# Hybrid decoder step: thirty 0/1-matrix sums as two products of a split operand, triangle matrices without their zero blocks, HGRN level products written together

## The chip, the cores and the metric

The kernel runs on one core of a Trainium2 chip. The metric is the device time of one execution in microseconds (us); lower is better. One execution was also profiled, and every row quoted below comes from it.

## The reference, cut to what matters

One trunk layer over 320 rows (256 of a prompt, 64 of eight samples), width 2048. All large matrices are float32.

```python
hn = rms_norm(x, norm_mix);  proj = hn @ w_in            # 2048 -> 6656 columns, three head groups
# A) RWKV-7: 12 heads of 64; delta rule with decay, in chunks here
kk = kf * k_k;  kk = kk / max(sqrt(sum(kk*kk, axis=-1)), 1e-12)          # sum over the 64 rows of a head
S = S*w + (S @ a) b^T + v k^T;  y = S @ r
mean = y.mean(-1); var = ((y-mean)**2).mean(-1)                           # sums over 64 rows
bonus = sum(r * k * r_k, axis=-1) * v                                     # sum over 64 rows
# B) HGRN2: 6 heads, 128 x 128 state
o = q exp(b) S + tril(q exp(b_t - b_s) k) v;  o = rms_norm(o, norm_w)     # sum over the 128 rows of a head
# C) RG-LRU: 512 channels
x = x + concat(y_rw, y_hg, y_lru) @ w_out
x = x + (silu(conv(gate)) * val) @ w_down                                 # gated MLP, width 5632
```

## The kernel before, in words

Data lies transposed: features on the 128 partitions, the 320 rows of tokens along the free dimension. Every large product is made exact enough by splitting: weights and activations are each cut into a rounded part (float32r) and the remainder, and a chunk of eight 128 x 128 weight tiles gives 24 products of 320 columns: high by high and low in turn (L198, L199), then low weights by high (L205). ScalarE (ACT) rounds the weights (L173), VectorE (DVE) subtracts (L174), SyncE (SP) loads them (L167).

The first third of the span ("the mixing stage") interleaves these products of `w_in` with the recurrences. The helper chains are Python generators: `tick` is called after every eight products and at a chunk's end, and lets a chain write its next step once the planner's clock has advanced by the amount that the chain yielded (`L_HG`, `L_EV`, `L_ST` and so on, in units near a microsecond). TensorE (PE) runs in the written order, apart from small shifts that the tile framework makes by readiness; every engine works its own queue in order.

The pieces that the change touches:

- **Sums over rows.** A sum over 64 or 128 partitions, broadcast back, is a product with a constant 0/1 matrix from the constant block `cst`: `bones` (same half of 64), `bswap` (other half), `ones`. There are five per pair of RWKV heads or HGRN head, six times: L502 (norm of k), L663 (bonus), L825 and L832 (mean and variance), L1019 (HGRN norm). These are products of plain float32 operands, 128 x 128 by 128 x 320. The three others with `ones` (L401, L1226, L1280 and L1281) sum over all features.
- **The triangle inverse.** Each RWKV pair needs the inverse of four 128 x 128 unit triangles that hold two 64 x 64 blocks, in tiles `mt1`, `Us`, `Ts`, `Z`. The 16 x 16 diagonal blocks are inverted by 30 small DVE instructions in sequence (L611, L613), for which `mt1` goes out to DRAM and comes back as blocks (L606, L607) and the result goes back the same way (L614, L615, all four from SP's queue). Then `Us` is transposed on PE (L686), and two levels of block products (L703) merge 16 to 32 and 32 to 64. Each such product has a 64 x 64 stationary block and 64 moving columns, of which half are zero by construction. ACT copies to `Z` (L708), DVE writes back under a mask (`update`, L695).
- **The chunk steps of RWKV.** Four chunks follow each other (L781, L784, L785 on PE; ACT and DVE make the state `sbd` in between at L792, L794), spaced by `L_ST`.
- **HGRN levels.** The intra-chunk matrix `at` of a head is filled level by level (h = 2, 4, ..., 64): `pairs` makes two or three products per level (L913, L917), each followed by its masked copy into `at` (L914, L918), all in one PSUM tile.
- **Transposes of v and kd** of a head go through a small tile `both` (L983), one buffer for each.

Of the kernel before, what the change touches and what calls it, by code (L numbers as in the profile page):

```python
# [51 lines left out]
CST = {}  # L52
_n = 0
for _name, _w in (
    ("ident", 128), ("ones", 128), ("bones", 128), ("bswap", 128), 
    ("psw", 128), ("eye2", 64), ("bmx", 4), ("bm4", 4), ("sel", 64), ("bm2", 2),
):
    CST[_name] = (_n, _w)
    _n += _w
# [7 lines left out]
def kernel(ctx: ExitStack, tc: tile.TileContext, i: dict, o: dict):  # L67
# [16 lines left out]
    prm = cp.tile([P, NPRM], F32, tag="prm", name="prm")  # L84
    cst = cp.tile([P, NCST], F32, tag="cst", name="cst")
    msk = cp.tile([P, NMSK], U8, tag="msk", name="msk")

    def pc(name, n, rows=slice(0, P)):
        c = PRM[name] + n
# [245 lines left out]
    G.memset(m01[:, 260:332:9], 0.0)  # L335

    ident = cc("ident")
    ones = cc("ones")

    def tok8(ap):  # L340
        return ap.rearrange("p (b t) -> p b t", t=ST)
# [100 lines left out]
        G.memset(t, 0.0)  # L442


    Zs = [mp.tile([P, 4, P], F32, tag=f"Z{h}", name=f"Z{h}") for h in (16, 32)]
    for Z in Zs:
        G.memset(Z, 0.0)

# [25 lines left out]
    def rwkv_operands(p, lw, box):  # L474
        while state["pairs"] < p - 1:
            yield None
        if p == 0:
            yield L_FIRST

        ps_w, ps_a = aux_r(), aux_r()  # L480
        for n, ps in enumerate((ps_w, ps_a)):
            PE.matmul(ps[:, :T], lw[half[n], n, :], lora[half[n], :], start=True, stop=True)  # L482
        sw = ft("sw")
        G.memset(sw[:, 0:260:65], 0.0)
        G.memset(sw[:, 260:332:9], 0.0)
        swp = sw[:, 0:260].rearrange("p (c s) -> p c s", s=65)
        sws = sw[:, 260:332].rearrange("p (c s) -> p c s", s=9)
        S.activation(swp[:, :, 1:65], ps_w[:, 0:TP].rearrange("p (c s) -> p c s", s=64), AF.Sigmoid,
                     bias=pc("w0", p))
        S.activation(sws[:, :, 1:9], tok8(ps_w[:, TP:T]), AF.Sigmoid, bias=pc("w0", p))  # L490
        a = ft("a", T)
        S.activation(a, ps_a[:, :T], AF.Sigmoid, bias=pc("a0", p))
        cum = ft("cum")
        V.tensor_tensor_scan(cum, m01, sw, 0.0, op0=ALU.mult, op1=ALU.add)
        while "k" not in box:
            yield None
        k, k_own = box["k"]
        kn = ft("kn", T)
        S.activation(kn, k, AF.Square, scale=pc("kk", p))
        yield L_K  # L500
        ps_k = aux_r()
        PE.matmul(ps_k[:, :T], cc("bones"), kn, start=True, stop=True)  # L502
        V.tensor_scalar(kn, ps_k[:, :T], 1e-24, None, op0=ALU.max)
        S.activation(kn, kn, AF.Ln, scale=float(2 ** 20))
        S.activation(kn, kn, AF.Exp, scale=-0.5, bias=eps_pow)  # L505
        ep = ft("ep")
        S.activation(ep, cum, AF.Exp, scale=-KAPPA)
        en = cum
        S.activation(en, cum, AF.Exp, scale=KAPPA)
        V.scalar_tensor_tensor(kn, k, pc("kk", p), kn, op0=ALU.mult, op1=ALU.mult)  # L510
        nb = ft("nb", T)
        V.scalar_tensor_tensor(nb, kn, -1.0, a, op0=ALU.mult, op1=ALU.mult)
        k2 = a
        V.tensor_scalar(k2, a, -1.0, pc("ka", p), op0=ALU.add, op1=ALU.mult)
# [48 lines left out]
    def rwkv_chunks(p, lw, box):  # L563
# [96 lines left out]
        state["samples"] += 1  # L660
        yield L_FILL
        ps_b = aux_r()
        PE.matmul(ps_b[:, :T], cc("bswap"), rk, start=True, stop=True)  # L663
        bo = ct("bo", T)
        V.tensor_tensor(bo, ps_b[:, :T], v, op=ALU.mult)
        free(v_own)
# [21 lines left out]
        for h, Z in zip((16, 32), Zs):  # L688
            def part(t, j):

                return t.rearrange("p b (n j s) -> p b n j s", j=2, s=h)[:, :, :, j, :]

            def update(t, name, j, ps):
                m = part(mask(name).unsqueeze(1), j)
                V.copy_predicated(part(t, j), m.to_broadcast([P, 4, 64 // h, h]),  # L695
                                  ps[:, 0:256].rearrange("p (b n s) -> p b n s", b=4, s=h))

            def blocks(ps, lhs, rhs, j):

                for b in range(4):  # L700
                    r = part(rhs[:, b:b + 1, :], j)
                    for q in half:
                        PE.matmul(ps[q, b * 64:(b + 1) * 64], lhs[q, b, q], r[q], start=True, stop=True)  # L703

            yield L_EV
            ps = aux_r()
            blocks(ps, mt1[:, 0], Ts, 0)
            S.copy(part(Z, 0), ps[:, 0:256].rearrange("p (b n s) -> p b n s", b=4, s=h))  # L708
            yield L_EV
            ps_u = aux_r()  # L710
            blocks(ps_u, Z, Us, 1)
            if h == 16:
                ps_t = aux_r()
                blocks(ps_t, Us, Z, 0)
            update(Us[:, 0:4, :], f"u{h}", 1, ps_u)
            if h == 16:
                update(Ts, "t16", 0, ps_t)

# [102 lines left out]
    def rwkv_norm(p, lw, y, bo):  # L821
        yield L_NORM

        ps_m = aux_r()
        PE.matmul(ps_m[:, :T], cc("bones"), y, start=True, stop=True)  # L825
        yc = ct("yc", T)
        V.scalar_tensor_tensor(yc, ps_m[:, :T], -1.0 / 64, y, op0=ALU.mult, op1=ALU.add)
        sq = ct("sqy", T)
        S.activation(sq, yc, AF.Square)
        yield L_EV  # L830
        ps_v = aux_r()
        PE.matmul(ps_v[:, :T], cc("bones"), sq, start=True, stop=True)  # L832
        lnv = sq
        S.activation(lnv, ps_v[:, :T], AF.Ln, scale=1.0 / 64, bias=eps_ln)
        S.activation(lnv, lnv, AF.Exp, scale=-0.5)
# [41 lines left out]
    def hgrn_steps(n, box):  # L877
# [28 lines left out]
        def pairs(lhs, rhs, h, w):  # L906

            ps = aux_h()
            for c0 in range(0, w, P):
                c = slice(c0, min(c0 + P, w))  # L910
                n = c.stop - c0
                if h == 2:
                    PE.matmul(ps[0:n, c], lhs[:, c], rhs[:, c], start=True, stop=True)  # L913
                    V.copy_predicated(at[0:n, c], mask("u2")[0:n, 0:n], ps[0:n, c])  # L914
                else:
                    o = ps[0:n, c0 // 2:(c0 + n) // 2]
                    PE.matmul(o, lhs[:, c], halves(rhs[:, c], n, h)[1], start=True, stop=True)  # L917
                    V.copy_predicated(halves(at[0:n, c], n, h)[1], halves(mask(f"u{h}")[0:n], n, h)[1],  # L918
                                      o.rearrange("p (n s) -> p n s", s=h))

# [56 lines left out]
        vt = rp.tile([P, 3, P], F32, tag="vt", name="vt", bufs=1)  # L977
        kt = rp.tile([P, 3, P], F32, tag="kt", name="kt", bufs=1)

        both = []  # L980
        for src in (v, kd):
            t = rp.tile([P, 2, TS], F32, tag="both", name="both", bufs=2)
            G.tensor_copy(t, bcast(src[:, TP:T], 2))  # L983
            both.append(t)
        for src, t, dst in ((v, both[0], vt), (kd, both[1], kt)):
            yield L_HG
            ps = aux_h()
            for m in range(2):
# [27 lines left out]
        S.activation(sq, ps_o[:, :T], AF.Square)  # L1016
        yield L_EV
        ps_n = aux_h()
        PE.matmul(ps_n[:, :T], ones, sq, start=True, stop=True)  # L1019
        rs = ht("hrs", T)  # L1020
        S.activation(rs, ps_n[:, :T], AF.Ln, scale=1.0 / P, bias=eps_norm)
        S.activation(rs, rs, AF.Exp, scale=-0.5)
# [278 lines left out]
L_NORM = 2.5  # L1301
L_FILL = 1.0
L_EV = 1.5
L_ST = 0.5
L_END = 0.5
L_HG = 2.0
L_HG0 = 12.0
# [23 lines left out]
def _constants():  # L1331
# [6 lines left out]
        c[:, CST[name][0]:CST[name][0] + CST[name][1]] = a.reshape(P, -1)  # L1338

    put("ident", (s == t).astype(f))  # L1340
    put("ones", np.ones((P, P), f))
    put("bones", (s // 64 == t // 64).astype(f))
    put("bswap", (s // 64 != t // 64).astype(f))
    s6 = (r % 64)[:, None]
    t6 = np.arange(64)[None, :]
    strict, causal = s6 < t6, s6 <= t6
# [120 lines left out]
```

## Time and profile before

| | |
|---|---|
| time, median of 3 runs | 1633.42 us (1631.91 to 1633.76) |
| the profiled execution: its own time | 1633.52 us |
| its span (first to last instruction) | 1631.8 us, so 1.7 us lie around it |
| granted TensorE clock | 0.997 |
| ACT table loads | 87, 111.6 us in all |
| DMA | 238.91 MB, mean 146 GB/s |

A matmul's row shows when it started and how long it took until its last result; since matmuls are pipelined, what one costs is the distance of starts, not its length. A plain float32 product appears as two records, a float32r product as one. "PEld" is the loading of stationary operands, which runs ahead of the products.

### The profile page before, as it was taken

What the parts mean: (1) busy time and instruction counts of PE and PEld (TensorE: products, weight loads), DVE (VectorE), ACT (ScalarE), POOL (GpSimd) and SP (SyncE); (2) the same over time, 40 slices, a digit from 0 to 9 for tenths busy, and PEclk for the clock granted to TensorE, in tenths of its full rate; (3) what the DMA queues carried; (4) which work ended last, traced back from release to release, by engine and by line L of the source; (5) the groups of instructions that cost most, each with busy time, mean ns of one, the idle gap of its engine ahead of it and who ended that gap; (6) DMA issues with size and microseconds to landing.
All of it is one profiled execution on the core that took longest, in us unless ns stands there. A gap on an engine that the chain in (4) does not pass through costs nothing.

```text
span 1631.8 us, 28987 instructions
## 1 busy us (share of the span) xinstructions
PE 1604.3 (98%) x11478; PEld 1549.6 (95%) x11478; DVE 984.9 (60%) x1965; ACT 821.9 (50%) x1289; POOL 147.9 (9%) x364
## 2 busy tenths in 40 slices
PE   9999999999999999999999999999999999999996
PEld 8888988888889999999999999999999999999996
DVE  7777787777777665555555554434555555554444
ACT  7766666767676774443443433332343443344442
POOL 2101110101011300011111100000011110010000
PEclk9999999999999999999999999999999999999998
DMA  7444342525353554444544445555444444545553
GB/s 267 151 131 133 119 137 92 159 94 158 96 153 114 166 165 153 153 152 147 155 146 152 147 150 146 151 148 151 155 155 145 153 145 154 154 147 156 146 153 108
DMA packets 87792, 238.91 MB, mean 146 GB/s; under 512 B 16713, under 2 KB 31097, under 8 KB 87657
## 3 DMA queue, kind: packets, MB, share of 16 engines
q1 hardware_dynamic: 81496, 221.01, 44.1%
q0 software_dynamic: 4576, 14.16, 2.6%
q8 instruction: 90, 1.47, 0.4%
q10 hardware_dynamic: 1584, 1.89, 0.3%
q14 instruction: 46, 0.37, 0.1%
HBM read 225.66 MB, written 11.37 MB: 145 GB/s over the span
## 4 chain that ended last, share of the span: by engine, by line
PE 89%; DVE 5%; ACT 4%; issue 1%; DMA 1%; SPq 0%; DVEq 0%; ACTq 0%
PE acc L198 27%; PE acc L205 27%; PE acc L199 26%; DMA raw<-in_w_in 1%; PE aux_r L703 1%; PE aux_h L917 1%; DVE wl L174 1%; ACT wh L173 0%; DVE x L1287 0%; PE aux_h L913 0%; PE aux_h L1046 0%; PE aux_r L781 0%; ACT L505 0%; PE aux_r L482 0%; PE aux_r L578 0%
## 5 line engine op out<-in xcount | busy, mean ns | idle before, releaser
L173 ACT CAST wh<-raw 128x1024 fp32r<-128x1024 f32 (+2 forms) x412 | 421.5, 1024 | 515.2 <-PE acc L199 310.9
L198 PE MATMUL acc<-xh,wh 128*128 128x320 f32 x2192 | 661.2, 315 | 0.0
L199 PE MATMUL acc<-xl,wh 128*128 128x320 f32 x2192 | 650.4, 310 | 0.0
L174 DVE TENSOR_TENSOR wl<-raw,wh 128x1024 fp32r<-128x1024 f32 (+2 forms) x412 | 489.6, 1189 | 228.6 <-ACT wh L173 113.4
L198 PEld LDWEIGHTS acc<-xh,wh 128*128 128x128 f32 x2192 | 411.6, 188 | 8.0 <-issue 5.5
L199 PEld LDWEIGHTS acc<-xl,wh 128*128 128x128 f32 x2192 | 412.0, 188 | 1.2
L205 PE MATMUL acc<-xh,wl 128*128 128x320 f32 x2192 | 375.6, 313 | 0.8 <-DVE wl L174 0.8
L205 PEld LDWEIGHTS acc<-xh,wl 128*128 128x128 f32 x2192 | 331.9, 188 | 6.8 <-issue 3.0
L198 PE MATMUL acc<-hh,wh 128*128 128x320 f32 x704 | 207.9, 308 | 0.0
L199 PE MATMUL acc<-hl,wh 128*128 128x320 f32 x704 | 207.8, 308 | 0.0
L199 PEld LDWEIGHTS acc<-hl,wh 128*128 128x128 f32 x704 | 132.2, 188 | 0.0
L198 PEld LDWEIGHTS acc<-hh,wh 128*128 128x128 f32 x704 | 131.6, 187 | 0.0
L205 PE MATMUL acc<-hh,wl 128*128 128x320 f32 x704 | 118.8, 308 | 0.0
L1249 POOL COPY ncch<-fe 128x18 f32<-128x18 f32 x44 | 49.6, 1128 | 653.1 <-DVE fe L1248 653.1
L205 PEld LDWEIGHTS acc<-hh,wl 128*128 128x128 f32 x704 | 107.1, 187 | 0.0
L1259 DVE TENSOR_TENSOR fv<-acc,rstd 128x320 f32<-128x320 f32 x44 | 21.6, 492 | 98.5 <-PE acc L205 98.5
L1247 DVE TENSOR_TENSOR fe<-acc,rstd 128x256 f32<-128x256 f32 x44 | 18.7, 425 | 99.9 <-PE acc L205 99.9
L214 ACT CAST hh<-fv 128x320 fp32r<-128x320 f32 x44 | 20.3, 460 | 97.0 <-DVE fv L1261 97.0
L198 PE MATMUL acc<-yhl,wh 128*128 128x320 f32 x224 | 66.1, 310 | 0.5 <-ACT yhl L214 0.5
L199 PE MATMUL acc<-yhl,wh 128*128 128x320 f32 x224 | 66.1, 308 | 0.0
L1254 DVE SCALAR_TENSOR_TENSOR fc<-fe,prm,fc 128x336 f32<-128x336 f32 x88 | 49.8, 565 | 1.6
L1252 ACT ACTIVATE fc<-fe,prm 128x336 f32<-128x336 f32 x44 | 29.4, 669 | 35.6 <-DVE fe L1248 35.6
(416 smaller groups left out, 1650.1 us busy)
## 6 DMA issues: line engine op xcount, KB each, us to landing
raw<-in_w_up SPq DMA_DIRECT2D x176, 512.0 KB, 3.6
raw<-in_w_in SPq DMA_DIRECT2D x100, 512.0 KB, 3.9
raw<-in_w_dn SPq DMA_DIRECT2D x64, 512.0 KB, 3.6
raw<-in_w_out SPq DMA_DIRECT2D x32, 512.0 KB, 3.7
raw<-in_w_dn SPq DMA_DIRECT2D x32, 384.0 KB, 3.2
out_s_hgrn<-hs POOLq DMA_DIRECT2D x12, 256.0 KB, 2.8
xr<-in_xT SPq DMA_DIRECT2D x16, 160.0 KB, 4.1
hs<-in_hs POOLq DMA_DIRECT2D x10, 256.0 KB, 4.1
```

Of the source, the lines that this page charges most:

```text
L173: S.copy(wh[:, ks, :], raws[n][:, ks, :])
L174: V.tensor_tensor(wl[:, ks, :], raws[n][:, ks, :], wh[:, ks, :].bitcast(F32), op=ALU.subtract)
L198: PE.matmul(ps[:, :T], wh[:, k, :], xh[k0 + k], start=st, stop=False)
L199: PE.matmul(ps[:, :T], wh[:, k, :], xl[k0 + k], start=False, stop=False)
L205: PE.matmul(ps[:, :T], wl[:, k, :], xh[k0 + k], start=False, stop=en)
L214: S.copy(xh, src)
L703: PE.matmul(ps[q, b * 64:(b + 1) * 64], lhs[q, b, q], r[q], start=True, stop=True)
L1247: V.tensor_tensor(e[:, 2:258], ps[:, 0:TP], rstd[:, 0:TP], op=ALU.mult)
L1249: G.tensor_copy(ncch[:, j], e[:, 248:EX].rearrange("p (b s) -> p b s", s=10)[:, :, 8:10])
L1252: S.activation(c[:, 0:N], e[:, 0:N], AF.Identity, scale=pc("fw", 3 * j), bias=pc("fb", j))
L1254: V.scalar_tensor_tensor(c[:, 0:N], e[:, m:m + N], pc("fw", 3 * j + m), c[:, 0:N], op0=ALU.mult, op1=ALU.add)
L1259: V.tensor_tensor(val, ps[:, :T], rstd, op=ALU.mult)
```

## The change

It has five parts.

1. The thirty sums go through a new helper `sums`: the operand is split (ACT rounds a copy to `high`, DVE subtracts to `low`) and two float32r products with the 0/1 matrix accumulate in PSUM. `high` and `low` have one buffer each, shared by all sums. The 0/1 matrices are filled by POOL into a tile `summing` instead of coming with `cst`, which loses 384 columns (196,608 bytes) of its load. The three sums with `ones` over all features stay plain float32.
2. `Z` keeps 64 columns per block row instead of 128, and the block products take 32 moving columns instead of 64. The masked write-back becomes two instructions of 64 partitions each; the copy to `Z` halves.
3. `pairs` writes all products of a level first and the masked copies behind them.
4. `L_ST` is 1.5 instead of 0.5.
5. `both` has one buffer instead of two, and each copy into it is written with its transposes.

```diff
-    ("ident", 128), ("ones", 128), ("bones", 128), ("bswap", 128), 
+    ("ident", 128),
...
+    summing = cp.tile([P, 3, P], F32R, tag="summing", name="summing")
+    ones = summing[:, 0, :].bitcast(F32)
...
+    G.memset(ones, 1.0)
+    for n in range(2):
+        for h in range(2):
+            for w in range(2):
+                G.memset(summing[h * 64:h * 64 + 64, 1 + n, w * 64:w * 64 + 64].bitcast(F32), float((h == w) == (n == 0)))
+
+    def sums(ps, n, src):
+
+        high = rp.tile([P, T], F32R, tag="high", name="high", bufs=1)
+        low = rp.tile([P, T], F32R, tag="low", name="low", bufs=1)
+        split(src, high, low)
+        PE.matmul(ps[:, :T], summing[:, n, :], high, start=True, stop=False)
+        PE.matmul(ps[:, :T], summing[:, n, :], low, start=False, stop=True)
...
-    Zs = [mp.tile([P, 4, P], F32, tag=f"Z{h}", name=f"Z{h}") for h in (16, 32)]
+    Zs = [mp.tile([P, 4, 64], F32, tag=f"Z{h}", name=f"Z{h}") for h in (16, 32)]
...
-        PE.matmul(ps_k[:, :T], cc("bones"), kn, start=True, stop=True)
+        sums(ps_k, 1, kn)
...
+            def diag(t):
+
+                return [t[q, 0:4, q] for q in half]
+
             def update(t, name, j, ps):
-                m = part(mask(name).unsqueeze(1), j)
-                V.copy_predicated(part(t, j), m.to_broadcast([P, 4, 64 // h, h]),
-                                  ps[:, 0:256].rearrange("p (b n s) -> p b n s", b=4, s=h))
+                for q, d in zip(half, diag(t)):
+                    m = part(mask(name)[q, q].unsqueeze(1), j)
+                    V.copy_predicated(part(d, j), m.to_broadcast([64, 4, 32 // h, h]),
+                                      ps[q, 0:P].rearrange("p (b n s) -> p b n s", b=4, s=h))
 
             def blocks(ps, lhs, rhs, j):
 
                 for b in range(4):
-                    r = part(rhs[:, b:b + 1, :], j)
-                    for q in half:
-                        PE.matmul(ps[q, b * 64:(b + 1) * 64], lhs[q, b, q], r[q], start=True, stop=True)
+                    for q, x, y in zip(half, lhs, rhs):
+                        PE.matmul(ps[q, b * 32:(b + 1) * 32], x[:, b, :], part(y[:, b:b + 1, :], j), start=True, stop=True)
...
             ps = aux_h()
+            outs = []
             for c0 in range(0, w, P):
                 c = slice(c0, min(c0 + P, w))
                 n = c.stop - c0
+                o = ps[0:n, c] if h == 2 else ps[0:n, c0 // 2:(c0 + n) // 2]
+                PE.matmul(o, lhs[:, c], rhs[:, c] if h == 2 else halves(rhs[:, c], n, h)[1], start=True, stop=True)
+                outs.append((c, n, o))
+            for c, n, o in outs:
                 if h == 2:
-                    PE.matmul(ps[0:n, c], lhs[:, c], rhs[:, c], start=True, stop=True)
-                    V.copy_predicated(at[0:n, c], mask("u2")[0:n, 0:n], ps[0:n, c])
+                    V.copy_predicated(at[0:n, c], mask("u2")[0:n, 0:n], o)
...
-L_ST = 0.5
+L_ST = 1.5
```

What this does to the order on the engines is seen at three places. Line numbers of the kernel after are larger than before by 3 near the start and by up to 22 in the HGRN part; L611 and L613 become L626 and L628, L703 becomes L722, L913 and L917 become L934.

On PE, the second level of an HGRN head (the fourth) reads before as follows. `qk` is the level's operand, `acc` the running product of `w_in`:

```order
L703 MATMUL aux_r<-T,mt_3804 64x64 x8
L917 MATMUL aux_h<-qk 128x64
L198 MATMUL acc<-xh_201,wh 128x320
L199 MATMUL acc<-xl_202,wh 128x320
L198 MATMUL acc<-xh_205,wh 128x320
L917 MATMUL aux_h<-qk 128x64
L199 MATMUL acc<-xl_206,wh 128x320
L198 MATMUL acc<-xh_209,wh 128x320
L199 MATMUL acc<-xl_210,wh 128x320
L198 MATMUL acc<-xh_213,wh 128x320
L917 MATMUL aux_h<-qk 64x32
```

Each of the three products stands between large products there. The same level after, on PE:

```order
L208 MATMUL acc<-xh_245,wl 128x320
L208 MATMUL acc<-xh_249,wl 128x320
L934 MATMUL aux_h<-qk 128x64 x2
L934 MATMUL aux_h<-qk 64x32
L201 MATMUL acc<-xh_147,wh 128x320
```

The three products of the level now stand together, with none of the large products between them.

On PE, the merge of 16 to 32 in one of the later pairs reads before as follows (`U`, `Z`: the inverse's tiles):

```order
L199 MATMUL acc<-xl_249,wh 128x320
L703 MATMUL aux_r<-U,Z_287 64x64 x8
L703 MATMUL aux_r<-Z_287,U 64x64 x8
L917 MATMUL aux_h<-qk 128x64
L205 MATMUL acc<-xh_201,wl 128x320
```

After the change the same merge on PE has the norm of k's sum (`high`, `low`) around and inside it:

```order
L352 MATMUL aux_r<-high,summing 128x320
L202 MATMUL acc<-xl_207,wh 128x320
L201 MATMUL acc<-xh_210,wh 128x320
L202 MATMUL acc<-xl_211,wh 128x320
L201 MATMUL acc<-xh_214,wh 128x320
L202 MATMUL acc<-xl_215,wh 128x320
L722 MATMUL aux_r<-U,Z_297 64x32 x8
L722 MATMUL aux_r<-Z_297,U 64x32 x2
L353 MATMUL aux_r<-low,summing 128x320
L722 MATMUL aux_r<-Z_297,U 64x32 x6
L981 MATMUL aux_h<-qk 128x128
```

The two products of a sum stand apart, and the second falls into the middle of a group of block products.

On DVE, inside the inversion of the 16 x 16 blocks of the fourth pair, the chain of 30 (`t`, `u`) reads before:

```order
L613 TENSOR_TENSOR u_3830<-u_3830,t_3831 40x7x9
L611 TENSOR_TENSOR t_3831<-n_3829,u_3830 40x60
L613 TENSOR_TENSOR u_3830<-u_3830,t_3831 40x6x10
L611 TENSOR_TENSOR t_3831<-n_3829,u_3830 40x55
L613 TENSOR_TENSOR u_3830<-u_3830,t_3831 40x5x11
L611 TENSOR_TENSOR t_3831<-n_3829,u_3830 40x48
L613 TENSOR_TENSOR u_3830<-u_3830,t_3831 40x4x12
```

The same stretch of DVE's queue after the change has other rows between the steps of the chain:

```order
L628 TENSOR_TENSOR u_4017<-u_4017,t_4018 40x7x9
L938 COPY_PREDICATED at<-msk,aux_h 64x64
L626 TENSOR_TENSOR t_4018<-n_4016,u_4017 40x60
L974 TENSOR_TENSOR qk<-hq,e 128x16x8
L628 TENSOR_TENSOR u_4017<-u_4017,t_4018 40x6x10
L975 TENSOR_TENSOR b<-b 128x16x8
L626 TENSOR_TENSOR t_4018<-n_4016,u_4017 40x55
L970 TENSOR_TENSOR x<-b 128x8x16
L628 TENSOR_TENSOR u_4017<-u_4017,t_4018 40x5x11
L997 TENSOR_TENSOR eb<-hq,eb 128x4x16
L626 TENSOR_TENSOR t_4018<-n_4016,u_4017 40x48
L883 TENSOR_TENSOR hg<-acc,rstd 128x320
```

Between the first and the last row of this chain stood 8 other rows before; after the change there are 29, most of them HGRN's.

More of the change, by code (lines that the diff above doesn't have):

```diff
@@ L337 @@
     ident = cc("ident")
-    ones = cc("ones")
+    G.memset(ones, 1.0)
[9 more added lines that the diff above has]
+        PE.matmul(ps[:, :T], summing[:, n, :], low, start=False, stop=True)
     def tok8(ap):
@@ L662, in rwkv_chunks @@
         ps_b = aux_r()
-        PE.matmul(ps_b[:, :T], cc("bswap"), rk, start=True, stop=True)
+        sums(ps_b, 2, rk)
         bo = ct("bo", T)
@@ L691, in part @@
                 return t.rearrange("p b (n j s) -> p b n j s", j=2, s=h)[:, :, :, j, :]
+            def diag(t):
+                return [t[q, 0:4, q] for q in half]
             def update(t, name, j, ps):
-                m = part(mask(name).unsqueeze(1), j)
-                V.copy_predicated(part(t, j), m.to_broadcast([P, 4, 64 // h, h]),
-                                  ps[:, 0:256].rearrange("p (b n s) -> p b n s", b=4, s=h))
+                for q, d in zip(half, diag(t)):
+                    m = part(mask(name)[q, q].unsqueeze(1), j)
+                    V.copy_predicated(part(d, j), m.to_broadcast([64, 4, 32 // h, h]),
+                                      ps[q, 0:P].rearrange("p (b n s) -> p b n s", b=4, s=h))
             def blocks(ps, lhs, rhs, j):
                 for b in range(4):
-                    r = part(rhs[:, b:b + 1, :], j)
-                    for q in half:
-                        PE.matmul(ps[q, b * 64:(b + 1) * 64], lhs[q, b, q], r[q], start=True, stop=True)
+                    for q, x, y in zip(half, lhs, rhs):
+                        PE.matmul(ps[q, b * 32:(b + 1) * 32], x[:, b, :], part(y[:, b:b + 1, :], j), start=True, stop=True)
+            zs = [Z[q] for q in half]
             yield L_EV
             ps = aux_r()
-            blocks(ps, mt1[:, 0], Ts, 0)
-            S.copy(part(Z, 0), ps[:, 0:256].rearrange("p (b n s) -> p b n s", b=4, s=h))
+            blocks(ps, diag(mt1[:, 0]), diag(Ts), 0)
+            S.copy(part(Z, 0), ps[:, 0:P].rearrange("p (b n s) -> p b n s", b=4, s=h))
             yield L_EV
             ps_u = aux_r()
-            blocks(ps_u, Z, Us, 1)
+            blocks(ps_u, zs, diag(Us), 1)
             if h == 16:
                 ps_t = aux_r()
-                blocks(ps_t, Us, Z, 0)
-            update(Us[:, 0:4, :], f"u{h}", 1, ps_u)
+                blocks(ps_t, diag(Us), zs, 0)
+            update(Us, f"u{h}", 1, ps_u)
             if h == 16:
@@ L824, in rwkv_norm @@
         ps_m = aux_r()
-        PE.matmul(ps_m[:, :T], cc("bones"), y, start=True, stop=True)
+        sums(ps_m, 1, y)
         yc = ct("yc", T)
@@ L831, in rwkv_norm @@
         ps_v = aux_r()
-        PE.matmul(ps_v[:, :T], cc("bones"), sq, start=True, stop=True)
+        sums(ps_v, 1, sq)
         lnv = sq
@@ L911, in pairs @@
                 n = c.stop - c0
+                o = ps[0:n, c] if h == 2 else ps[0:n, c0 // 2:(c0 + n) // 2]
+                PE.matmul(o, lhs[:, c], rhs[:, c] if h == 2 else halves(rhs[:, c], n, h)[1], start=True, stop=True)
+                outs.append((c, n, o))
+            for c, n, o in outs:
                 if h == 2:
-                    PE.matmul(ps[0:n, c], lhs[:, c], rhs[:, c], start=True, stop=True)
-                    V.copy_predicated(at[0:n, c], mask("u2")[0:n, 0:n], ps[0:n, c])
-                else:
-                    o = ps[0:n, c0 // 2:(c0 + n) // 2]
-                    PE.matmul(o, lhs[:, c], halves(rhs[:, c], n, h)[1], start=True, stop=True)
+                    V.copy_predicated(at[0:n, c], mask("u2")[0:n, 0:n], o)
+                else:
                     V.copy_predicated(halves(at[0:n, c], n, h)[1], halves(mask(f"u{h}")[0:n], n, h)[1],
@@ L978, in hgrn_steps @@
         kt = rp.tile([P, 3, P], F32, tag="kt", name="kt", bufs=1)
-        both = []
-        for src in (v, kd):
-            t = rp.tile([P, 2, TS], F32, tag="both", name="both", bufs=2)
+        for src, dst in ((v, vt), (kd, kt)):
+            t = rp.tile([P, 2, TS], F32, tag="both", name="both", bufs=1)
             G.tensor_copy(t, bcast(src[:, TP:T], 2))
-            both.append(t)
-        for src, t, dst in ((v, both[0], vt), (kd, both[1], kt)):
             yield L_HG
@@ L1018, in hgrn_steps @@
         ps_n = aux_h()
-        PE.matmul(ps_n[:, :T], ones, sq, start=True, stop=True)
+        sums(ps_n, 0, sq)
         rs = ht("hrs", T)
@@ L1340, in _constants @@
     put("ident", (s == t).astype(f))
-    put("ones", np.ones((P, P), f))
-    put("bones", (s // 64 == t // 64).astype(f))
-    put("bswap", (s // 64 != t // 64).astype(f))
     s6 = (r % 64)[:, None]
```

## The prediction

> **What bounds the kernel.** First the page's chain of waits, then busy time by stage (length; then PE, PEld, DVE, ACT and POOL, with record counts; clock, DMA share, GB/s).
>
> ```profile
> PE 89%; DVE 5%; ACT 4%; issue 1%; DMA 1%; SPq 0%; DVEq 0%; ACTq 0%
> 50.00:600.00 550.00, 538.72 (x4271) 489.83 (x4272) 420.74 (x1142) 387.74 (x735) 74.92 (x188) 1.00 0.42 129
> 700.00:1620.00 920.00, 918.72 (x6259) 917.70 (x6258) 461.07 (x661) 352.61 (x431) 58.89 (x126) 1.00 0.48 147
> ```
>
> PE ends last in both stages, at full clock; the change touches only the first, the mixing stage. There DVE is busy 420.74 of 550 us and ACT 387.74: they have room for more work, but not for being late. So the change is worth the PE starts that it saves, plus the waits of PE's queue that go, less those that come. The waits show best at the weight loads, which PE's queue meets first (sum in us, times, longest):
>
> ```profile
> PEld aux_r L781 <- DVE sbd L794: 4.4, 5, 2.3
> PEld aux_h L913 <- DVE at L914: 3.1, 6, 1.9
> PEld aux_h L917 <- DVE at L918: 3.0, 5, 0.9
> PEld aux_r L502 <- ACT kn L499: 1.6, 1, 1.6
> ```
>
> **The sums.** PE in order of time (start, length), around one sum and around eight large products:
>
> ```profile
> 79.75 1.34 PE L205 MATMUL acc<-xh,wl 128*128 128x320 f32 x8
> 80.92 0.31 PE L198 MATMUL acc<-xh,wh 128*128 128x320 f32 x1
> ...
> 103.28 0.70 PE L502 MATMUL aux_r<-kn,cst 128*128 128x320 f32 x2
> 103.58 0.55 PE L198 MATMUL acc<-xh,wh 128*128 128x320 f32 x1
> 103.97 0.31 PE L199 MATMUL acc<-xl,wh 128*128 128x320 f32 x1
> ```
>
> Eight float32r products of 320 columns take 80.92 - 79.75 = 1.17 us of starts, 0.146 each. The sum and one large product take 103.97 - 103.28 = 0.69, so the sum costs 0.54. Two float32r products of the same size cost 0.29. Five sums, six times: 30 x 0.25 = **-7.4 us**. Their splits go to ACT and DVE, here priced by the same operation on `yhl` (columns: busy sum, then mean ns):
>
> ```profile
> L214 ACT CAST yhl<-yo 128x320 fp32r<-128x320 f32 x16 | 6.9, 457 | 1.8 <-PE aux_r L762 0.9 <-DVE yo L1151 0.8
> L215 DVE TENSOR_TENSOR yhl<-yo,yhl 128x320 fp32r<-128x320 f32 x16 | 7.5, 481 | 0.0
> ```
>
> 30 x 0.46 = 14 us on ACT and 30 x 0.48 = 14 us on DVE fit into the 160 and 130 us that they idle in this stage. But every sum's second product now waits 0.94 us longer for its operand, in a queue where the large products stand behind it. The order puts 2 to 16 large products (0.3 to 2.3 us) in front as cover. Bounds: nothing, if cover always holds, and 30 x 0.94 = 28 us if never. Most covers are longer than the split, so I take a seventh of it, **+4**.
>
> **Triangles.** Two groups of eight block products, the first followed by another kind, the next two by each other, and the exit of a group:
>
> ```profile
> 100.71 0.31 PE L199 MATMUL acc<-xl,wh 128*128 128x320 f32 x1
> 100.95 0.68 PE L703 MATMUL aux_r<-T,mt 64*64 64x64 f32 x16
> 101.56 0.43 PE L917 MATMUL aux_h<-qk 128*128 128x64 f32 x2
> ...
> 105.09 0.68 PE L703 MATMUL aux_r<-U,Z 64*64 64x64 f32 x16
> 105.60 0.63 PE L703 MATMUL aux_r<-Z,U 64*64 64x64 f32 x16
> ...
> 356.42 0.45 PE L762 MATMUL aux_r<-bkt,pq 64*64 64x64 f32 x12
> 356.80 0.41 PE L198 MATMUL acc<-xh,wh 128*128 128x320 f32 x1
> 357.05 0.31 PE L199 MATMUL acc<-xl,wh 128*128 128x320 f32 x1
> ```
>
> A group takes 105.60 - 105.09 = 0.51, eight steps of 0.064, since two records of the two halves run side by side. Whether half the moving columns shorten a step, the rows of HGRN tell, with a full stationary operand and 128 or 64 moving columns:
>
> ```profile
> 82.10 0.38 PE L913 MATMUL aux_h<-e,f 128*128 128x128 f32 x2
> 82.24 0.39 PE L198 MATMUL acc<-xh,wh 128*128 128x320 f32 x1
> 82.47 0.31 PE L199 MATMUL acc<-xl,wh 128*128 128x320 f32 x1
> ...
> 88.02 0.33 PE L917 MATMUL aux_h<-qk 128*128 128x64 f32 x2
> 88.16 0.39 PE L198 MATMUL acc<-xh,wh 128*128 128x320 f32 x1
> 88.39 0.30 PE L199 MATMUL acc<-xl,wh 128*128 128x320 f32 x1
> ```
>
> Both take 0.37 with one large product, 0.22 alone: below 128 moving columns something else sets the pace, here 0.11 per record. I read it as the load of 128 stationary columns; for 64 of them that is 0.055 a step, hardly below the 0.064 of now. Bounds: nothing, and half of every group, 30 x 0.25 = 7.5 us. I go by the HGRN pair and take one step's half per group, 30 x 0.03 = **-0.8**. The Trainium skill ("TensorE: Matmul & The Clock Gate", section "LDWEIGHTS (loading the stationary operand)") says that a load takes the stationary columns over 1.2 GHz, whatever the rows, an estimate of 53 ns for 64 columns; the two rows above agree. The same page's section "Back-to-back issue gap" gives moving columns over 2.4 GHz plus 2.5 ns; by that rule alone the sum would be 7 us lower, which is a rival below.
>
> Entering a group with part of the array costs 100.95 - 100.71 = 0.24 instead of 0.146, its tail 0.61 instead of 0.51, leaving it 0.25 (356.80 to 357.05) instead of 0.146: 0.3 in all. In PE's order such groups number 97 before and 101 after (five merges are cut by a `low`, three cuts of L755 by an HGRN product go): 4 x 0.3 = **+1.2**. The masked write-backs become twice as many rows of half the partitions, 18 more on DVE, and the copy to `Z` halves; both engines' idle time holds them.
>
> **HGRN and chunk steps.** Products written together cost the same 0.22 each; what goes is the wait of a second chunk for the first one's copy, 3.1 + 3.0 in the waits above. First chunks still wait for their operand, so 1.6 of it stays: **-4.5**. With `L_ST` 1.5, 16 large products (2.3 us) instead of 8 (1.2) lie between chunk steps, and the wait for `sbd` was 4.4 in five events of at most 2.3: **-4.0**. L502's 1.6 was one event; its place moves two groups of eight later: **-1.0**. Bounds for the three: 0 and 13.
>
> **What comes late next.** The inversion on DVE. One pair (fourth), DVE, SP's DMA issues and PE, then the landing time of `U` (KB each, us):
>
> ```profile
> 299.74 2.48 DVE L584 TENSOR_TENSOR mt<-aux_r,msk 128x512 f32<-128x512 f32 x4
> 308.94 0.16 DVE L611 TENSOR_TENSOR t<-n,u 40x15 f32<-40x15 f32 x1
> 312.05 0.20 DVE L611 TENSOR_TENSOR t<-n,u 40x55 f32<-40x55 f32 x1
> 312.28 0.21 DVE L613 TENSOR_TENSOR u<-u,t 40x55 f32<-40x55 f32 x1
> 312.41 0.47 DVE L665 TENSOR_TENSOR bo<-aux_r,xs 128x320 f32<-128x320 f32 x1
> 312.81 0.20 DVE L611 TENSOR_TENSOR t<-n,u 40x60 f32<-40x60 f32 x1
> 319.88 0.17 DVE L613 TENSOR_TENSOR u<-u,t 40x15 f32<-40x15 f32 x1
> 323.04 0.38 SPq L615 DMA_DIRECT2D U<-du  x1
> 330.25 0.60 PE L686 MATMUL aux_r<-cst,U 128*128 128x128 f32 x4
> U<-du SPq DMA_DIRECT2D x6, 320.0 KB, 3.9
> ```
>
> The chain of 30 lasts from 308.94 to 320.05, 11.1 us; `U` lands at 323.04 + 3.9 = 326.9 and PE needs it at 330.25: 3.3 us to spare. After the change 29 other rows instead of 8 stand inside. They don't cost their full length: a dependent step follows after its length plus 0.03 (312.05 + 0.20 to 312.28), an independent one 0.07 to 0.08 before the end (312.41 + 0.47 to 312.81). By the durations of their lines, the 30 own rows sum to 5.9 us and the 29 others to 12.2; less 59 x 0.08 that is 13.4, so 2.3 more. PE's place for L686 comes about 0.4 earlier after L578 (an estimate: the rows between the two in both orders, at the prices above), and DVE starts L584 about 0.5 later, since one row of 0.48, a `low`, is new ahead of it. That leaves 0.1 us to spare, and the chain now also holds rows that wait for PE's products (L914's and L918's copies) and ACT's exponentials. Bounds: 0, and 6 x 4.6 = 28 us (below). I take 0.5 a head, **+3**; and **+1** for other new waits (one `both` buffer: its refill has 16 large products of cover).
>
> `cst`'s smaller load and POOL's nine fills end before the first sum and price at nothing; the feed-forward stage is untouched.
>
> **Sum**: -7.4 + 4 - 0.8 + 1.2 - 4.5 - 4.0 - 1.0 + 3 + 1 = -8.5. The profiled execution took 1633.5 us (span 1631.8 and 1.7 around it), 0.1 above the median of 1633.4: **1625.0 us**.
>
> **Rivals.** (a) The triangles run at the pace of moving columns: 7.5 instead of 0.8, so 7 more, 1618. For it: 0.064 is also what two passes of 64 columns take at 0.146 per 320 (0.058). Against it: L917 beside L913. (b) The splits eat the gain: high and low behind cover too short in 18 of 30 sums, 0.7 each instead of the 4 in all: 13 - 4 = 9 more, 1634, no change. For it: DVE and ACT take a weight split of over 1 us in between at any time. (c) **Slower**: the inversion gets late in every head. If other rows cost their full length on DVE, the chain takes 18.1 instead of 13.4, `U` lands 4.7 later, and less the 0.1 to spare PE stands 4.6 at L686, six times: 28 instead of 3, 1650. It decides from a wait of 1.9 us a head ((8.5 + 3) / 6), where the whole gain is gone. Against it: rows 312.41 and 312.81.
>
> **Chances.** Forecast 0.60 (its own range 1617 to 1631), (a) 0.14, (b) 0.13, (c) 0.13. The range 1612 to 1636 leaves out (c) and the end where (a) meets no new wait at all. Within 0.2% (3.3 us, about what a measurement can tell) falls most of (b), 0.10; slower is (c), 0.13; faster 0.77.
>
> **What would show it.** Right: the five sums' rows become records at 0.146 without idle time before them, the wait for `sbd` under 1 us in sum, two records of L722 side by side at 0.055 to 0.064. Wrong: steps near 0.03 (a); idle time before the `low` products (b); L686's successor waiting for the DMA of `U`, its landing more than 31 us after L584 (c).

## The result: slower, and the profile after

| | |
|---|---|
| time after, median of 4 runs | 1656.01 us (1654.94 to 1658.13) |
| time before on the same chip, median of 4 runs | 1633.59 us (1631.91 to 1634.43) |
| ratio after to before | 1.0139, 95% interval 1.0126 to 1.0151 |
| span of the profiled execution after | 1656.3 us |
| granted TensorE clock over that span | 0.988 (before 0.997) |
| ACT table loads | 88 (before 87) |

The forecast was 1625.0 us, range 1612 to 1636. The time is 22 us above the kernel before and outside the range.

The chain of waits and the mixing stage of the kernel after, in the columns of before:

```profile
PE 82%; ACT 7%; DVE 6%; DMA 2%; issue 2%; SPq 0%; POOL 0%; DVEq 0%; ACTq 0%
50.00:600.00 550.00, 519.95 (x4120) 475.65 (x4119) 413.07 (x1164) 381.02 (x738) 75.09 (x177) 0.98 0.40 124
```

PE's share of the chain fell from 89 to 82%. In the same 550 us it is busy 19 us less than before, and its clock is 0.98 instead of 1.00. DVE and ACT are busy no longer than before. So nothing new is full, and PE waits. For what, the waits at the weight loads say (sum in us, times, longest):

```profile
PEld aux_r L662 <- ACT sqy L854: 13.5, 5, 2.7
PEld aux_r L749 <- issue: 11.2, 5, 2.2
PEld aux_r L801 <- DVE sbd L814: 5.3, 6, 1.2
PEld aux_r L352 <- POOL at L916: 2.6, 1, 2.6
```

Two places are new, once in each of five pairs: L662 (the transposes of `bks`, L647 before), which need a PSUM tile that ACT's Ln of the variance L854 (L834) reads, and L749 (the products with `U`, L729). In the view of PE itself the second one is put down to DVE's write-back into `U` (10.0 us). The rows of the sums, L352 and L353, wait long only once, at the first sum (2.6 us). POOL's fill of `at`, which the view names there, is no operand of that product. Its operand `high` is, and on ACT the cast to it stood behind a table load and ended at 53.56; PE went on at 53.71:

```profile
51.35 1.28 ACT L522 ACT_TABLE_LOAD   x1
...
53.12 0.44 ACT L217 CAST high<-kn 128x320 fp32r<-128x320 f32 x1
```

The landing of `U`, the place of the slower rival, is not among them: PE waited 0.7 us in all for it (L701).

**The clock goes with the waits.** PE around the wait at L662 in one pair, and the granted clock there (window, busy PE, PEld, DVE, ACT, POOL, then clock):

```profile
156.59 0.30 PE L202 MATMUL acc<-xl,wh 128*128 128x320 f32 x1
159.33 0.45 PE L662 MATMUL aux_r<-cst,BKs 128*128 128x128 f32 x2 [2.44 <-ACT sqy L854]
...
160.65 0.47 PE L201 MATMUL acc<-xh,wh 128*128 128x320 f32 x1
160.92 0.47 PE L202 MATMUL acc<-xl,wh 128*128 128x320 f32 x1
...
164.70 0.31 PE L201 MATMUL acc<-xh,wh 128*128 128x320 f32 x1
164.85 0.31 PE L202 MATMUL acc<-xl,wh 128*128 128x320 f32 x1
```

```profile
160.00:162.50 2.50, 2.50 (x10) 2.38 (x9) 1.15 (x5) 2.49 (x6) 0.00 (x0) 0.50 0.00 0
```

Behind the wait the large products start 0.27 us apart (160.65 to 160.92) instead of 0.15 (164.70 to 164.85), at half the clock. Over the whole stage, in 220 windows of 2.5 us, the sum of (1 - clock) x 2.5 is 13.7 us, in eight groups of windows; before there is none. The waits of 2.0 us and more are eleven (five, five and the first sum), and eight of them have such a group behind them. So a wait of that kind cost its own length and, in eight of eleven cases, about 1.7 us more.

**Why L662 is late.** ACT in order of time, ahead of that wait:

```profile
150.38 0.44 ACT L217 CAST high<-sqy 128x320 fp32r<-128x320 f32 x1
...
151.75 1.28 ACT L913 ACT_TABLE_LOAD   x1
...
155.10 1.28 ACT L954 ACT_TABLE_LOAD   x1
156.40 0.34 ACT L954 ACTIVATE e<-x 128x160 f32<-128x160 f32 x1
...
157.45 1.28 ACT L854 ACT_TABLE_LOAD   x1
158.75 0.53 ACT L854 ACTIVATE sqy<-aux_r,eps_t 128x320 f32<-128x320 f32 x1
```

ACT's queue holds the Ln of the next HGRN head (L913), its Exps (L954, L955), and only then the Ln of the variance (L854), since the cast to `high` at 150.38 and DVE's subtraction now stand between the square and the sum. Ln and Exp sit in different tables here, so each change costs a load of 1.28 us, and this Ln pays one of its own. PE's transposes wait for it till 159.33.

**Why L749 is late.** ACT and DVE at the norm of k of the pair after it, then PE (start, length):

```profile
192.44 0.27 ACT L982 COPY a<-aux_h 128x128 f32<-128x128 f32 x1 [2.32 <-PE aux_h L981]
192.73 1.28 ACT L519 ACT_TABLE_LOAD   x1
...
194.51 1.28 ACT L520 ACT_TABLE_LOAD   x1
195.80 0.56 ACT L520 ACTIVATE kn<-kn,eps_t 128x320 f32<-128x320 f32 x1
...
197.21 0.25 ACT L728 COPY Z<-aux_r 128x128 f32<-128x128 f32 x1
```

```profile
191.56 0.49 DVE L518 TENSOR_SCALAR kn<-aux_r 128x320 f32<-128x320 f32 x1 [0.27 <-PE aux_r L353]
...
196.40 0.55 DVE L525 SCALAR_TENSOR_TENSOR kn<-xs,prm,kn 128x320 f32<-128x320 f32 x1 [3.13 <-ACT kn L520]
...
203.35 0.30 DVE L715 COPY_PREDICATED U<-msk,aux_r 64x128 f32<-64x128 uint8 x1
```

```profile
194.68 0.66 PE L722 MATMUL aux_r<-T,mt 64*64 64x32 f32 x16
...
198.09 0.66 PE L722 MATMUL aux_r<-U,Z 64*64 64x32 f32 x16
198.68 0.43 PE L740 MATMUL aux_r<-vs,mt 128*128 128x64 f32 x2
...
203.80 1.87 PE L749 MATMUL aux_r<-rq,U 128*128 128x128 f32 x8 [2.00 <-DVE U L715]
```

The last level of the triangle inverse is caught in both queues. Its first product ends at 195.34, but the copy to `Z` stands behind the two table loads of the norm of k and runs at 197.21. Its second product ends at 198.75, but the write-back to `U` stands on DVE behind everything that waited 3.13 us for the same norm, and ends at 203.65. PE stands in front of L749 till 203.80.

### The profile page after: what moved, and what is told of

It is laid out like the page before. It is cut to its first block, busy times and chain, and to the rows that moved or that the text cites. A ratio compares the mean times of both kernels' runs of the same rounds, so it can differ in the third digit from the quotient of the medians.

```text
span 1656.3 us, 29092 instructions
## 1 busy us (share of the span) xinstructions
PE 1607.1 (97%) x11478; PEld 1556.1 (94%) x11478; DVE 991.1 (60%) x2013; ACT 831.4 (50%) x1320; POOL 151.2 (9%) x373
## 4 chain that ended last, share of the span: by engine, by line
PE 82%; ACT 7%; DVE 6%; DMA 2%; issue 2%; SPq 0%; POOL 0%; DVEq 0%; ACTq 0%
PE acc L201 25%; PE acc L202 25%; PE acc L208 24%; DVE wl L177 2%; ACT wh L176 1%; PE aux_h L934 1%; DMA raw<-in_w_in 1%; PE aux_r L722 1%; DMA U<-du 0%; PE aux_r L749 0%; ACT L854 0%; ACT L913 0%; ACT L954 0%; ACT L1040 0%; ACT L519 0%
## 5 line engine op out<-in xcount | busy, mean ns | idle before, releaser
L201 PEld LDWEIGHTS acc<-xh,wh 128*128 128x128 f32 x2192 | 415.2, 189 | 13.7 <-issue 11.9
L208 PE MATMUL acc<-xh,wl 128*128 128x320 f32 x2192 | 370.8, 311 | 0.0
```

The costliest lines, as they stand in the source:

```text
L201: PE.matmul(ps[:, :T], wh[:, k, :], xh[k0 + k], start=st, stop=False)
L208: PE.matmul(ps[:, :T], wl[:, k, :], xh[k0 + k], start=False, stop=en)
```

## The experiments

Experiments of one round were run together with the kernel before; "before" is its median there. All numbers are medians, with the 95% interval of the ratio.

### First round: which part of the change

Three theories: P, the place (with `L_ST` 1.5 the RWKV chains stand 56 large products later, amid HGRN's table loads); S, the split sums make the chains late; G, the grouping of HGRN's products.

The edits, each against the kernel after (the second against the kernel before):

```diff
e1:  -L_ST = 1.5
     +L_ST = 0.5
e2:  -L_ST = 0.5
     +L_ST = 1.5
e3, in sums:
-        high = rp.tile([P, T], F32R, tag="high", name="high", bufs=1)
-        low = rp.tile([P, T], F32R, tag="low", name="low", bufs=1)
-        split(src, high, low)
-        PE.matmul(ps[:, :T], summing[:, n, :], high, start=True, stop=False)
-        PE.matmul(ps[:, :T], summing[:, n, :], low, start=False, stop=True)
+        PE.matmul(ps[:, :T], summing[:, n, :].bitcast(F32), src, start=True, stop=True)
e4:  pairs as before: each product followed by its masked copy
```

> The changed kernel with L_ST back at 0.5, all else as changed. Theory P (place): L_ST 1.5 moves every RWKV chain 56 large products later against the products of w_in, so that the Ln of the variance and the makers of the next pair's operands fall into an HGRN head's start, where ACT changes tables; then this gives back nearly all: 1620 to 1632 us, with the waits at L662 (13.5 us) and L749 (11.2) under 3 us together. Theory S (split): the two-step sums themselves make the chains late; then the time stays above 1645. Theory G (grouping): the HGRN products written together take DVE or PE at the wrong time; then it also stays above 1645.

> The kernel before with L_ST 1.5 alone. P: slower than before, 1645 to 1660 us, with new waits of several us behind ACT's tables. S and G: no slower than before, 1627 to 1634, since only the 4.4 us of waits for sbd go.

> The changed kernel with the thirty sums as single plain float32 products again (the 0/1 matrices still filled by POOL). P: it stays slow, and PE does 7.4 us more work: 1655 to 1668. S: back to the time before or near, 1630 to 1640, although PE does more. G: 1655 to 1668, as P.

> The changed kernel with the HGRN products each followed by its masked copy again, as before. P: stays slow, 1652 to 1665 (the waits between chunks return, up to 5 us). S: the same. G: 1625 to 1640.

| run (before 1635.15) | us | ratio |
|---|---|---|
| e1, after with `L_ST` 0.5 | 1646.74 | 1.0068 [1.0051, 1.0085] |
| e2, before with `L_ST` 1.5 | 1636.83 | 1.0016 [1.0006, 1.0025] |
| e3, after with plain sums | 1625.63 | 0.9941 [0.9926, 0.9956] |
| e4, after with the old `pairs` | 1661.20 | 1.0159 [1.0144, 1.0175] |

The theory of the place (P) misses by its times: the late place alone costs the kernel before 1.7 us (a little more than S and G had expected, far less than P), and the early place leaves the kernel after 11 us slower than the kernel before, though 9 us faster than with the late place. But one sign of P came true. In e1 the two new waits are nearly gone:

```profile
PEld aux_r L749 <- issue: 2.2, 1, 2.2
PEld aux_r L662 <- ACT uv L649: 0.7, 1, 0.7
```

So these two waits need the split and the late place together: e1 (split, early) has only one of 2 us left, e2 and e3 (late, no split) have none. e1 has other waits instead, the longest of them 3.1 us, once, for the cast of a weight on ACT; what makes them isn't shown.

The grouping (G) is no loss, it is worth 5 us even here. What makes the kernel slower is the split of the sums (S): without it the same kernel is 30 us faster, more than S had expected, and beats the kernel before. Its mixing stage:

```profile
50.00:600.00 550.00, 545.06 (x4334) 498.70 (x4335) 420.11 (x1166) 378.45 (x731) 69.26 (x186) 1.00 0.43 133
```

Between e3 and the kernel after, PE's idle time in this stretch differs by 545.06 - 519.95 = 25.1 us and the slow clock by 13.7 us. Less the 7.4 us of work that the split was forecast to save, that is 31.4. The first product of `w_out` starts at 596.11 us in the kernel after and at 564.45 in e3, so the mixing stage of these two profiled executions differs by 31.7 (the medians of the times by 30.4). In PE's view the two waits are 12.2 + 10.0 = 22.2 of the 25.1 us. They and the clock behind the waits account for most of the loss.

### Second round: which of the sums

```diff
e6 (variance):   -        sums(ps_v, 1, sq)
e7 (norm of k):  -        sums(ps_k, 1, kn)
e9 (both and the mean): the same for ps_k, ps_m and ps_v
+        PE.matmul(ps_v[:, :T], summing[:, 1, :].bitcast(F32), sq, start=True, stop=True)
e8:  -L_NORM = 2.5
     +L_NORM = 2.0
```

> The kernel after, with only the variance sum of the RWKV norm (six of the thirty) taken as one plain float32 product again; the other 24 stay split. Theory V (one place): in the kernel after, the split puts an ACT copy and a DVE subtraction between the square and the variance sum, so on ACT the Ln of the variance stands behind the Ln and the Exps of the next HGRN head; that costs two more table loads per pair (1.28 us each) and holds the PSUM tile for which TensorE waits at the transposes of bks, and the late inversion that follows from it makes the wait at the product with U as well. In the order of this kernel the Ln of the variance stands right behind HGRN's Ln and ahead of its Exps. V expects both waits (12.2 and 10.0 us over five pairs) gone, 78 table loads and 1624 to 1630 us. Theory K (two places): the wait at U comes from the split of the norm of k, which makes DVE wait for ACT; then only the wait at the transposes goes: 1637 to 1645 us, with about 10 us left at U. Theory D (spread over all splits): a fifth of the 30 us returns, 1648 to 1652 us.

> The kernel after, with only the sum for the norm of k (six of the thirty) taken as one plain float32 product; the other 24 stay split. In its order on ACT the Ln of the variance stands behind HGRN's Exps as in the kernel after, with 88 table loads. V expects no change: 1653 to 1659 us, both waits as after. K expects the wait at U (10.0 us, and the slow products behind it) gone: 1640 to 1646 us. D expects 1648 to 1652 us.

> The kernel after with all thirty sums split, and L_NORM 2.0 instead of 2.5: the norm's chain is written one step earlier, so that on ACT the Ln and Exp of the variance stand ahead of HGRN's Ln and Exps (behind its Sigmoid) instead of behind them. Everything else, the 88 table loads and the work of every engine included, stays. V expects that the place in ACT's queue is what costs, not the splits or the number of loads: no wait at the transposes of bks, 1622 to 1634 us, faster than the kernel before or level with it. A theory by which the splits cost their time wherever they stand, or by which it is the number of table loads, expects 1650 to 1660 us.

> The kernel after, with the sums of the norm of k, the mean and the variance (eighteen) taken as plain float32 products and those of the bonus and of the HGRN norm (twelve) still split. These twelve feed no chain that TensorE waits for soon. If their splits are covered, their saved work (12 times 0.25 us, 3 us) shows beside the variant with thirty plain sums (1625.6 us): 1621 to 1624 us. If they aren't covered, or if covers are worth as much as the work, 1625 to 1630 us. D expects 12/30 of the 30 us: 1636 to 1639 us.

| run (before 1634.10) | us | ratio |
|---|---|---|
| e6, variance plain | 1639.94 | 1.0038 [1.0024, 1.0051] |
| e7, norm of k plain | 1639.97 | 1.0037 [1.0022, 1.0051] |
| e8, all split, norm one step earlier | 1670.57 | 1.0227 [1.0212, 1.0242] |
| e9, norm of k, mean and variance plain | 1628.28 | 0.9964 [0.9952, 0.9976] |

The waits at the weight loads of e6, which has two of the kernel after's, and of e7, which has one:

```profile
PEld aux_r L749 <- issue: 11.2, 5, 2.2
PEld aux_r L662 <- ACT uv L649: 6.5, 5, 1.3
```

```profile
PEld aux_r L662 <- ACT sqy L854: 13.5, 5, 2.7
```

One place (V) is refuted, and so is an even spread (D): each of the two sums has its own wait and is worth 16 us. With the variance plain the wait at L749 stays to the digit, and that at L662 halves; with the norm of k plain L749 is gone from the list and L662 stays to the digit. That is theory K. In e6 the Ln and the Exp of the variance follow an Ln and an Exp of the HGRN head with no change of table between, so they need no load of their own: it has 78 table loads, the kernel after 88. In e7 the norm of k looks like this on ACT and DVE:

```profile
183.39 1.28 ACT L519 ACT_TABLE_LOAD   x1
184.68 0.47 ACT L519 ACTIVATE kn<-kn 128x320 f32<-128x320 f32 x1
...
186.47 0.56 ACT L520 ACTIVATE kn<-kn,eps_t 128x320 f32<-128x320 f32 x1
...
189.40 0.27 ACT L728 COPY Z<-aux_r 128x128 f32<-128x128 f32 x1 [1.19 <-PE aux_r L722]
```

```profile
184.01 0.48 DVE L518 TENSOR_SCALAR kn<-aux_r 128x320 f32<-128x320 f32 x1
...
194.55 0.61 DVE L715 COPY_PREDICATED U<-msk,aux_r 64x128 f32<-64x128 uint8 x2
```

The first table load begins at 183.39, before the sum is there (DVE ends L518 at 184.49), so it is covered; in the kernel after ACT stood at the copy of `a` till 192.44 and loaded the table behind it. From the end of L518 to the end of the Exp it takes 2.5 us here and 4.3 there (192.05 to 196.36). The copy to `Z` now waits for PE and not for ACT's queue.

e8 is the instructive miss. The Ln of the variance did move ahead of HGRN's, as its order had it, and the time got worse. In ACT's order of time, all of this now stands in front of the copy L649, which frees PSUM for L662:

```profile
236.61 1.28 ACT L854 ACT_TABLE_LOAD   x1
...
238.71 1.28 ACT L855 ACT_TABLE_LOAD   x1
...
240.50 1.28 ACT L913 ACT_TABLE_LOAD   x1
...
243.36 1.28 ACT L954 ACT_TABLE_LOAD   x1
...
245.73 0.20 ACT L649 COPY uv<-aux_r 64x64 f32<-64x64 f32 x1
```

PE waited 4.0 us there, five times, by its own view of the waits. So an earlier place of the Ln doesn't help by itself: now four loads, 5.1 us, stand ahead of the copy that PE needs, and the time lies above both forecasts. That it is the loads that cost is tested in the third round.

In e9 both waits are gone with twelve sums still split, but it isn't faster than e3 (0.9964 beside 0.9941, with intervals that overlap a little). Of the expected 3 us nothing is seen; its wait for `sbd` at the chunk steps is 7.5 us where e3 has 3.7. The HGRN norm, still split there, has an Ln and an Exp with a load each too (L1040, L1041), in ACT's queue ahead of copies to `sbd`; that they make this wait is not shown.

### Third round: table loads or latency, and the other parts by themselves

```diff
e13, against after:
-        S.activation(kn, kn, AF.Ln, scale=float(2 ** 20))
-        S.activation(kn, kn, AF.Exp, scale=-0.5, bias=eps_pow)
+        S.activation(kn, kn, AF.Identity, scale=0.01)
+        S.activation(kn, kn, AF.Identity, scale=0.01)
...
-        S.activation(lnv, ps_v[:, :T], AF.Ln, scale=1.0 / 64, bias=eps_ln)
-        S.activation(lnv, lnv, AF.Exp, scale=-0.5)
+        S.activation(lnv, ps_v[:, :T], AF.Identity, scale=0.01)
+        S.activation(lnv, lnv, AF.Identity, scale=0.01)
e14: e13 with the plain sums of e3
e10: e3 with Z, blocks and update as before the change
e11: e3 with pairs as before the change
e12: e3 with L_ST = 0.5
```

> The kernel after with all thirty sums split. Left out: the Ln and the Exp of the norm of k and of the variance; in their places stand plain scalings on ACT (Identity, scale 0.01), as many instructions of the same size, which need no table. ACT's order keeps the two places as they are in the kernel after (the copy of a ahead of the norm of k, the second copy to Z behind it; the variance behind HGRN's Exps), but there are 64 table loads instead of 88. Theory T: each late chain costs TensorE time because the table loads (two of 1.28 us at the norm of k, two at the variance) stand in ACT's queue ahead of the copies that TensorE waits for, so a split's added step of about 1 us would be covered without them. T expects the waits at the transposes of bks (12.2 us) and at the product with U (10.0 us) to shrink to a third or less, and 1618 to 1632 us. Theory L: the split's own latency (cast on ACT, subtraction on DVE) makes the chains late and the loads only stand by: both waits stay above two thirds, 1645 to 1656 us.

> As the variant without tables (Ln and Exp of the norm of k and of the variance left out, plain scalings in their places, 64 table loads; 1624.6 us, 0.9937 of the kernel before), but with all thirty sums as plain float32 products. Beside it the worth of the split alone is seen, with nothing late behind table loads. If the saving forecast for TensorE is real and its cover holds: 5 to 8 us slower than with the split, 1630 to 1633 us. If the splits' waits eat it (the variant with split sums still waits 4.6 us at the transposes of bks): 1622 to 1626 us. If the splits cost even then: under 1622 us.

> The kernel after with all thirty sums as plain products (1625.6 us in its run), and the triangles as before: Z with 128 columns, 64 moving columns in each block product, one masked copy of 128 partitions. If a block product costs the loading of its stationary block, as forecast (0.8 us for all six pairs): 1625 to 1628 us. If the narrower products, the halved copy to Z or the shorter masked copies shorten the inverse where TensorE waits for it: 1629 to 1634 us. If the two masked copies per update cost more than one: 1621 to 1624 us.

> The kernel after with all thirty sums as plain products, and the HGRN levels as before: each product followed by its masked copy. Forecast for the grouping: 4.5 us less waiting at the second product of a level and 1.2 us more for changes of the array's part, so 3 to 4 us of the gain of the plain variant: 1628 to 1631 us. With the split sums in place the grouping was worth 5 us (1661.2 beside 1656.0). If it is worth nothing here: 1625 to 1627 us.

> The kernel after with all thirty sums as plain products and L_ST 0.5. In its order the RWKV chains stand where they stood before, and ACT has 87 table loads as before instead of 78. Forecast for L_ST 1.5: 4 us less waiting at the chunk steps, so 1629 to 1631 us without it. If the place of the chains is what L_ST 1.5 brings (the variance's Ln and Exp share their tables with HGRN's, 10 loads fewer) and that is worth more than the chunk steps: 1632 to 1640 us. If L_ST is worth nothing, as it was in the kernel before (1636.8 beside 1635.2): 1624 to 1627 us.

| run | us | ratio |
|---|---|---|
| e13, all split, 24 table loads left out | 1624.55 | 0.9937 [0.9923, 0.9950] |
| e14, all plain, the same loads left out | 1628.80 | 0.9963 [0.9949, 0.9977] |
| e10, plain sums, old triangles | 1626.34 | 0.9947 [0.9934, 0.9959] |
| e11, plain sums, old `pairs` | 1634.13 | 0.9998 [0.9989, 1.0007] |
| e12, plain sums, `L_ST` 0.5 | 1630.08 | 0.9969 [0.9957, 0.9980] |

(Before 1634.47, for e14 1634.94.) e13 and e14 leave out the Ln and the Exp of two norms, so they don't compute the reference; they only show what the loads cost. The mixing stage of e13 and its largest wait of this kind:

```profile
50.00:600.00 550.00, 537.96 (x4332) 496.52 (x4331) 432.48 (x1197) 370.06 (x748) 78.99 (x186) 1.00 0.43 133
```

```profile
PEld aux_r L662 <- ACT sqy L854: 5.9, 5, 1.2
```

With every split in place and the loads gone, the whole loss comes back and more (1624.6 beside 1656.0): the wait at L749 vanishes, the clock is 1.00 in every window, and the wait at L662 falls from 13.5 to 5.9 (theory T had asked for a third; it is 0.44). Theory L, which had asked for more than two thirds at both places, is refuted. What is left at L662 is not all the split's: e14, with no split at all, still waits 3.6 there.

e14 shows the other term. Beside it the split is worth 4.2 us by the medians (0.9963 - 0.9937 of 1634), less than the 5 to 8 that were forecast. Up to the first product of `w_out` PE is busy 549.64 us in e13 and 556.87 in e14, so the saved work is 7.2 us in the profiled executions; PE idles 13.6 and 13.0 us in them. The saving was there all along, 4 to 7 us of the 7.4. One thing isn't explained: e14 is slower than e3, though it has fewer table loads (64 beside 78). It waits 3.6 us at the transposes and 3.3 us for the landing of `U`, where e3 has 1.4 and 0.5.

## Why the prediction was wrong, step by step

- **What bounds the kernel**: right. PE's starts and PE's waits carry the time, and DVE and ACT have "room for more work, but not for being late". The trouble is that the next steps priced lateness at one place only.
- **The sums, -7.4**: right in mechanism, 4 to 7 by e13 beside e14.
- **The splits, +4**: this is the step that failed. "Most covers are longer than the split, so I take a seventh" asks whether the sum's own product finds cover in PE's queue, and nearly always it does: L352 and L353 wait long only at the first sum. What counts is who reads the sum. Three of the five feed an Ln and an Exp on ACT. For two of these, the norm of k and the variance, a delay of a microsecond moved them behind other instructions in ACT's order. At the norm of k this exposed a table load that is covered in e7, at the variance it added two loads per pair, and both held up copies of other chains that queue behind them. The two waits also need the late place that `L_ST` 1.5 gives (e1); the prediction priced the two parts apart. e3 beside the kernel after is 30.4 us; with the 4 to 7 saved, the split cost some 35 to 38, more than the bound of 28 (no cover at all). Neither the loads, 111.6 us in the table of before, nor the clock were a term of the sum.
- **Triangles, -0.8**: 0.7 by e10, too small to tell from nothing. Rival (a), 7.5 us, is out: a group of eight takes 198.68 - 198.09 = 0.59 in the kernel after and 0.61 before, ahead of a product on the full array. Half the moving columns bring hardly anything here.
- **HGRN grouping, -4.5**: 8.5 by e11, nearly twice the forecast. The waits of the kernel before were 3.1 at L913 (the products of the first level) and 3.0 at L917. With `L_ST` 1.5 and the old `pairs` nearly all of it is at the first level, in e2 and in e11 (L929 there):

```profile
PEld aux_h L913 <- DVE at L914: 6.6, 6, 1.9
PEld aux_h L929 <- DVE at L930: 6.4, 6, 1.6
```

e3 has no such wait, where the forecast left 1.6. So the grouping takes away 6.4; the other 2 us of the 8.5 aren't explained.

- **`L_ST`, -4.0**: 4.5 by e12, so the number is right, but the mechanism only in part. The wait for `sbd` was to fall under 1 us; it falls from 6.1 in e12 to 3.7 in e3, and is 5.3 in the kernel after. What the other 2 us are isn't shown (e12 has 87 table loads, e3 78). In the kernel before `L_ST` 1.5 costs 1.7 (e2), and e11, with `L_ST` 1.5 and the old `pairs`, is level with the kernel before. So it seems to pay only beside the grouping; no run has plain sums with `L_ST` 0.5 and the old `pairs` to show it.
- **L502, -1.0**: not gained. The first sum still waits 1.3 us in e3, and 2.6 in the kernel after. The +1.2 for entering and leaving groups and the +1 for other new waits were not measured by themselves.
- **The inversion, +3, and rival (c)**: refuted. PE waited 0.7 us for the landing of `U`. The slower result came from two other queues, so that (c)'s 1650 lies near the measured time is luck. Rival (b), covers too short in the sums themselves, named the right part of the change and the wrong place; no change was its price.
- **Without the split**, the forecast's remaining terms sum to -5.1, and e3 measured -9.5. Taken out of e3 one at a time, triangles, grouping and `L_ST` are worth 0.7 + 8.5 + 4.5 = 13.7, so the parts don't add up singly.

e13 and e14 aside, which leave out the Ln and the Exp of two norms, e3 is the fastest: the change with plain sums, 1625.63 us, 0.9941 of the kernel before.

## What to carry to other kernels

Where an operation is made longer on a helper engine, follow its result to the next instruction of an in-order queue that loads a table or waits, and list what stands behind that instruction; price those, not the operation. A saving of 0.25 us thirty times is lost to ten waits of 2.0 to 2.4 us. Once a chain's order on ACT changes, count the table loads between an operand and the copies that TensorE needs, since moving one of them earlier can hold up more (e8). Price two parts of a change together where one moves the chain that the other makes longer (e1, e3).

## What the hardware showed that was not expected

**The clock often falls after waits of 2 us.** Eight of the eleven waits of 2.0 us and more in the kernel after were followed by two or three windows of 2.5 us with a clock of 0.50 to 0.93, 1.7 us lost each. It was two of five waits of 2.4 us in e7 and three of six of 2.0 us in e6. The one wait of 2.05 us in the kernel before was not followed by any, and in e3, e9 and e13, whose waits are shorter, no window of the stage is below 1.00. e8, with waits of 2.0 and of 4.0 us, five of each, lost 20.5 us in this way; all five of 4.0 us were followed by a slow clock. The Trainium skill ("TensorE: Matmul & The Clock Gate", section "What's actually happening") has the clock halve after an idle window of about 3.4 us and says that windows run freely, which could be why some waits are spared; the measured waits that were followed by half the clock are shorter than that, 2.0 to 2.5 us.

**A table load can be covered.** In e7 it ran ahead of its activation's operand: 1.28 us from 183.39, with the operand ready at 184.49 and the Ln at 184.68. The Trainium skill ("ScalarE: Activation LUTs", section "What ACT_TABLE_LOAD costs") gives about 2.66 us for a change of tables, the load and a drain. Here no drain shows: in the kernel after a load begins at 155.10 and its Exp at 156.40, 1.30 us later, and the instruction ahead of the load ends at 155.08.
